# Measured numbers in a schedule's model of times, and the rows of decays loaded through ScalarE's DMA queue

## The chip, the core and the metric

The kernel runs on one core of a Trainium2 chip. The metric is the time of one execution on the device in microseconds; the value for the kernel before is the median of three runs.

## What is computed

One inference step of a hybrid decoder layer for 256 prompt tokens and 8 sample tokens, which go together as 264 columns. One input projection makes the columns of three groups of heads: windowed attention, a pooling mixer and a gated delta rule. All mixed heads go through one output projection, and a last norm follows. Cut to what bears on this case:

```python
h = rms_norm(x, norm_w)
z = h @ w_in                                   # 4096 x 14368
# delta rule, per head: decays from the cumulated gates of a chunk
gc = jnp.cumsum(chunks(g), axis=-1)
decay = jnp.exp(jnp.where(causal, gc[..., :, None] - gc[..., None, :], -jnp.inf))
a_mat = jnp.where(strict, jnp.einsum('nbhid,nbhjd->nbhij', kb, kc) * decay, 0.0)
...
qk = jnp.einsum('nbhid,nbhjd->nbhij', qc, kc) * decay
...
y = x + concat(attention, pooling, delta rule) @ w_out
return rms_norm(y, final_norm_w), new caches and states
```

The old window caches are outputs too, moved on by one row: 128 MB of them are copied from HBM to HBM.

## The kernel before

**The stream.** Both projections are one stream of 145 output tiles of 128 rows (113 of `w_in`, 32 of `w_out`), each a sum over 32 contraction tiles. A chunk is 8 contraction tiles of one output tile. Weights come as float32 from HBM into three places (`raw`) through SyncE's DMA queue, 1 MB for two chunks. Each chunk is split into two parts that TensorE multiplies at full speed: ScalarE rounds it to the upper part (`wh`), VectorE subtracts that from the original to get the lower part (`wl`). Three matmuls of 264 columns a contraction tile make the product (lines 540 to 542). `wh` and `wl` have four buffers each (HB = 4), so the splits may be three chunks ahead of TensorE; `emit_split(n + HB - 1)` follows `emit_main(n)`. The last split of a load frees its place, and the next load is then written into the program (`emit_loads`, line 456), with a piece of the caches' copy now and then (`emit_copy`).

**The side chains.** Everything else is written as Python generators: taking output tiles out of PSUM (`ev_...`), `kk` (products of the keys with themselves, one chain a head), `invert` and `assemble`, two `delta_worker`s and two `sample_worker`s (heads one after another), attention and pooling. A chain yields where it can wait. `step` (line 1395) runs once a chunk, before the chunk's matmuls: each chain may go on by one step if VectorE and ScalarE have time for it beside the stream. Products of side chains wait in a list and are put into a later chunk by `flush` (line 321), at its last contraction tile (PE_AT).

**The planner.** All this is settled when the program is built, by an estimate of the engines' clocks. `Model` (line 75) holds a time for each engine and for each column's last write and use. `Meter` (line 144) prices an instruction: fixed part, part for each element, part for a column given as a scalar (on VectorE 0.07 + 0.00104 n + 0.06 us). `emit_main` adds a price for each contraction tile to TensorE's time. The limit in `step` is

```python
end = t["pe"] + extra + (HB - 1) * 2.72 - 1.27 - MARGIN
```

A step fits if VectorE's planned time stays below `end`, and ScalarE's 1.05 us below it. The planner orders the work; on the chip the semaphores do, so a wrong price costs a wait and nothing else.

**Queues.** Each engine runs its instructions in the order in which the program was written. SyncE issues nearly all DMAs (`self.sy` and `self.ld` are the same); an issue that has to wait holds all that is behind it. `Model.dma` (line 132) prices SyncE's transfers one after the other at 359 GB/s.

**The rows of decays.** `ev_ab` writes the cumulated gates of 16 heads to a scratch tensor in HBM (`s_gc`). `load_decay(h, gcb)` (line 719) reads one row of it, 256 values, onto all 128 partitions (128 KB). It is called twice a head: in `kk`, where `due` then holds the chain until the planner takes the load for landed (`self.loaded`), and in `delta`, where four steps lie between load and use. `decay` (line 722) uses it: two instructions on VectorE, an exponential on ScalarE.

Of the kernel before, what the change touches and what calls it, by code (L numbers as in the profile page):

```python
# [11 lines left out]
P = 128  # L12
NP = 256            # prompt tokens
NB = 8              # sample tokens (one per sequence)
NT = NP + NB
NK = 32             # contraction tiles of the model width
KC = 8              # contraction tiles per chunk
# [10 lines left out]
def tile_plan():  # L28
    """Order of the output tiles of the input projection: (kind, index)."""
    plan = [("ab", 0)] + [("k", h) for h in range(CH)]  # L30
    for h in range(CH):
        plan += [("q", h), ("v", h), ("g", h)]
    for h in range(AH):
        plan += [("qa", h), ("ka", h), ("va", h), ("ga", h)]
    for g in range(4):
        plan += [("u", 2 * g), ("u", 2 * g + 1), ("gb", 2 * g), ("gb", 2 * g + 1)]
    return plan
# [37 lines left out]
class Model:  # L75
    """Estimated times (us) of the engines' queues, and of every column's last write and last use."""
# [7 lines left out]
    def span(self, ap):  # L84
        """The quarters of the partitions and the columns of a tile (the kernel's inputs and outputs are not followed)."""
        name = ap.tensor.name
        if name in self.outside:
            return None
        if name not in self.written:
            n = 1  # L90
            for x in ap.tensor.shape[1:]:
                n *= x
            self.written[name], self.used[name] = np.zeros((4, n)), np.zeros((4, n))
        dims = list(ap.ap)
        n = self.written[name].shape[1]
        if dims[0][0] % n or ap.tensor.shape[0] != P:
            return name, np.s_[:, :]
        lo, p = ap.offset % n, ap.offset // n
        last = p + dims[0][0] // n * (dims[0][1] - 1)
        hi = lo + 1 + sum(st * (c - 1) for st, c in dims[1:])  # L100
        return name, np.s_[p // 32:last // 32 + 1, lo:hi]
# [15 lines left out]
    def op(self, eng, dur, outs, ins):  # L117
        t = max(self.t[eng], self.ready(outs, ins))
        # engines take turns at a PSUM bank
        banks = {x.tensor.name for x in [*outs, *ins] if x.tensor.name in self.banks}  # L120
        for n in banks:
            last, when = self.banks[n]
            if last != eng:
                t = max(t, when + self.LAG)
        t += dur
        for n in banks:
            self.banks[n] = (eng, t)
        self.t[eng] = t
        self.done(t, outs, ins)
        return t  # L130
# [13 lines left out]
class Meter:  # L144
    """An engine, with an estimate of the time that its instructions take (us)."""
# [5 lines left out]
    def __getattr__(self, name):  # L151
        f = getattr(self.eng, name)

        def run(*a, **k):
            if name == "dma_start":
                if self.key == "sy":
                    self.b.loaded = self.b.model.dma(k["out"], k["in_"])
                return f(*a, **k)  # L158
            names = ("in_", "in0", "in1", "data0", "data1", "scalar", "scalar1", "scalar2", "scale", "bias")
            ins = [k[x] for x in names if x in k and k[x] is not None and not isinstance(k[x], (int, float))]  # L160
            ins += [x for x in a[1:] if not isinstance(x, (int, float))]
            outs = [k["out"] if "out" in k else a[0]] + ([k["accum_out"]] if "accum_out" in k else [])
            ap = (ins or outs)[0]
            n = 1
            for x in ap.shape[1:]:
                n *= x
            ptr = any(k.get(x) is not None and not isinstance(k[x], (int, float)) for x in ("scalar", "scalar1", "scale", "bias"))
            dur = self.fixed + (self.each * n if name != "reciprocal" else .0065 * n) + (self.pointer if ptr else 0.0)
            if k.get("op") == ALU.pow:
                dur = .12 + .17 * n  # L170
            self.used += dur
            t = self.b.model.op(self.key, dur, outs, ins)
            self.b.cur.ready = max(self.b.cur.ready, t)
            return f(*a, **k)  # L174
# [4 lines left out]
class Chain:  # L179
    """A generator, the estimated time at which its last step is through, and its products yet to be issued."""  # L180
# [10 lines left out]
class Builder:  # L191
# [54 lines left out]
    def get_all(self, *sizes):  # L246
        """All of them or none, so that no two chains wait for each other's space."""
        while True:
            out = []
# [40 lines left out]
    def due(self, loaded):  # L290
        """Until a load can be expected to be there."""
# [7 lines left out]
    def lose(self, t):  # L299
        """Time for ScalarE's tables."""  # L300
# [4 lines left out]
    def mm(self, out, lhsT, rhs, start=True, stop=True):  # L305
        """A side product: it is issued inside a later chunk of the stream."""
# [14 lines left out]
    def flush(self, every=True):  # L321
        """The side products whose operands can be expected to be there."""
        for c in list(self.pending):
# [7 lines left out]
            c.later = []  # L331
            self.pending.remove(c)
# [4 lines left out]
            for bufs in done:  # L337
                self.free_now(*bufs)

# [57 lines left out]
    def late_const(self):  # L397
# [4 lines left out]
        # halves: silu(z) = (tanh(z/2) + 1) * z/2  # L402
        self.ts(self.cw, self.cw, 0.5, ALU.mult)
        # buffers of the delta-rule phase
# [12 lines left out]
    def setup_stream(self):  # L417
        self.chunks = []      # (m, first k tile, number of k tiles, load index, offset in the load's tiles)
        self.loads = []       # (m, first k tile, number of k tiles, last chunk served, place, load that frees it)
# [36 lines left out]
    def emit_loads(self, limit=None):  # L456
        """The loads whose place is free."""
# [54 lines left out]
    def main_bank(self, m):  # L512
        """The PSUM bank of an output tile, and the tile that had it before."""
# [4 lines left out]
    def emit_main(self, n):  # L518
# [3 lines left out]
        for i in range(nk):  # L522
# [5 lines left out]
            self.model.t["pe"] += .226 if m == 0 else .339  # L528
            xh, xl = self.rhs(m, k)
            w = slice(i * 128, (i + 1) * 128)  # L530
            if m == 0:
                # rows 0 to 63: W's upper part by x; rows 64 to 127: its lower part by x's upper part
# [22 lines left out]
    def square_x(self, q):  # L555
        """Squares of four of the k tiles, summed into self.ssum."""
# [103 lines left out]
    def ev_ab(self, ps):  # L660
# [13 lines left out]
        # a_log -> -exp(a_log)  # L674
# [44 lines left out]
    def load_decay(self, h, gcb):  # L719
        self.ld.dma_start(out=gcb.ap, in_=self.s_gc[h:h + 1, :].to_broadcast([P, NP]))  # L720

    def decay(self, h, gcb, D):
        """D[j, t, i] = exp(gc_i - gc_j) for i >= j, else 0."""
# [58 lines left out]
    def invert(self):  # L782
        """T = (I + A)^-1 of the 128 diagonal 32 x 32 blocks, one block per partition."""
# [32 lines left out]
    def assemble(self, hb):  # L816
        """E = T^T of the 128 x 128 tiles, from its 32 x 32 diagonal blocks, in place of U."""
# [90 lines left out]
    def delta(self, h, R, kd, D, o, S, X, sq):  # L908
# [65 lines left out]
        # 128 eps (sum q^2 + eps)  # L974
# [19 lines left out]
        # the last reader of k, U and E has been issued: their place takes the head's output  # L994
# [16 lines left out]
    def sample_tab(self):  # L1011
        """Columns by (head, sequence), then rows on all partitions: e^g, k2 e^g beta, k beta."""
# [156 lines left out]
    def have(self, k, buf):  # L1169
        """Row tile k of the mixed heads; those of attention come in two parts."""  # L1170
# [202 lines left out]
    def finish_early(self):  # L1373
        """What the last norm needs of the tiles but one."""
# [20 lines left out]
    def step(self, free=False):  # L1395
        """Each side chain goes on by a step, as far as VectorE and ScalarE have time beside the stream."""
# [3 lines left out]
        end = t["pe"] + extra + (HB - 1) * 2.72 - 1.27 - MARGIN  # L1400
# [83 lines left out]
    def build(self):  # L1484
# [8 lines left out]
        # TensorE's clock rises while it is busy  # L1493
# [113 lines left out]
# the first output tiles go side by side through the contraction, while x comes in  # L1607
# [4 lines left out]
# pieces of the caches' copy per load of weights: keys' tiles, delta rule, attention, pooling, output  # L1612
# [49 lines left out]
def _bias(count):  # L1662
    """A position that `count` patterns share, as an additive term of its unscaled score."""
# [11 lines left out]
def _layouts(inp):  # L1675
# [28 lines left out]
    for n, src in (("kg", "cache_win_k"), ("vg", "cache_win_v")):  # L1704
        g = f[src][0][:, rows]                                  # (8, 320, 8, 128)
# [44 lines left out]
```

## Time and profile before

| | us |
|---|---|
| median of three runs | 1834.63 |
| lowest and highest run | 1830.6 and 1837.5 |
| span of the profiled execution, first to last instruction | 1828.2 |
| what lies between the median and the span | 6.4 |
| TensorE busy | 1801.3 (99%) |
| VectorE busy | 1298.7 (71%) |
| ScalarE busy | 850.3 (47%) |
| DMA queue of SyncE, share of 16 DMA engines | 80.5% |

The span is the profiled execution's own time on the engines; its time by the clock of the runs isn't known apart, and the median stands for it. A matmul's recorded time is longer than its place in the stream: a 264-column matmul shows 0.28 us and the next one starts 0.12 after it. So busy time alone doesn't tell whether TensorE is at its full pace; the number of matmuls in a stretch does.

### The profile page before, as it was taken

The page shows a single profiled execution, that of the slowest core. Times are in us where ns is not written, and L with a number is a line of the kernel's source. Part 1 is how long each engine was busy: PE and PEld are TensorE (multiplying, and loading weights), DVE is VectorE, ACT ScalarE, POOL GpSimd, SP SyncE. Part 2 cuts the span into 40 slices and gives each one's busy share as a digit, 9 for nine tenths or more (in the row PEclk, how much of TensorE's full clock was granted, in tenths as well). Part 3 has the DMA queues.
Part 4 walks back from the last instruction along what each step waited for, and adds up shares of the span by engine and source line. Part 5 has one row for each costly group of instructions (what it writes and reads, how often), then busy time and mean ns, then how long its engine had stood idle before and what let it go on. Part 6 is the DMA issues. An engine that isn't in the chain of part 4 may idle for free.

```text
span 1828.2 us, 38217 instructions
## 1 busy us (share of the span) xinstructions
PE 1801.3 (99%) x15120; PEld 1790.3 (98%) x15120; DVE 1298.7 (71%) x3155; ACT 850.3 (47%) x1442; POOL 192.8 (11%) x504
## 2 busy tenths in 40 slices
PE   9999999999999999999999999999999999999996
PEld 9999999999999999999999999999999999999995
DVE  7987879668789788787877778676655654444444
ACT  7644444455455455455544443434333444444442
POOL 1132560421011101111000000000000000000000
PEclk9999999999999999999999999999999999999998
DMA  9788897656787888879888888889888798888873
GB/s 322 263 289 295 272 234 260 237 198 234 262 327 269 286 305 313 304 267 319 323 312 306 313 308 297 284 283 333 306 299 288 274 339 302 295 294 303 297 240 118
DMA packets 109380, 519.66 MB, mean 284 GB/s; under 512 B 25408, under 2 KB 35872, under 8 KB 70272
## 3 DMA queue, kind: packets, MB, share of 16 engines
q1 hardware_dynamic: 108624, 516.71, 80.5%
q8 instruction: 118, 1.93, 0.4%
q0 software_dynamic: 432, 0.50, 0.1%
q14 instruction: 62, 0.51, 0.1%
q10 hardware_dynamic: 144, 0.02, 0.0%
HBM read 499.67 MB, written 152.50 MB: 357 GB/s over the span
## 4 chain that ended last, share of the span: by engine, by line
PE 88%; DVE 5%; DMA 4%; issue 1%; ACT 1%; SPq 1%; DVEq 0%; ACTq 0%
PE mps L540 27%; PE mps L541 27%; PE mps L542 27%; PE sps L307 4%; DVE arena L174 3%; DMA raw<-win 3%; DVE wl L174 2%; PE sps L311 1%; PE sps L541 1%; PE sps L540 1%; PE sps L542 1%; SPq L158 1%; DVE y L174 1%; DMA o_ds<-arena 0%; ACT wh L174 0%
## 5 line engine op out<-in xcount | busy, mean ns | idle before, releaser
L540 PE MATMUL mps<-xh,wh 128*128 128x264 f32 x3456 | 995.3, 288 | 2.0 <-ACT wh L174 2.0
L542 PE MATMUL mps<-xh,wl 128*128 128x264 f32 x3456 | 979.9, 284 | 1.7 <-DVE wl L174 1.6
L174 DVE TENSOR_TENSOR wl<-raw,wh 128x1024 fp32r<-128x1024 f32 (+1 forms) x581 | 704.5, 1214 | 389.7 <-ACT wh L174 382.4
L541 PE MATMUL mps<-xl,wh 128*128 128x264 f32 x3456 | 980.2, 284 | 0.0
L174 ACT CAST wh<-raw 128x1024 fp32r<-128x1024 f32 (+2 forms) x586 | 604.8, 1036 | 611.2 <-PE mps L541 471.7
L540 PEld LDWEIGHTS mps<-xh,wh 128*128 128x128 f32 x3456 | 652.1, 189 | 3.7 <-ACT wh L174 2.5
L541 PEld LDWEIGHTS mps<-xl,wh 128*128 128x128 f32 x3456 | 651.7, 189 | 0.2
L542 PEld LDWEIGHTS mps<-xh,wl 128*128 128x128 f32 x3456 | 648.8, 188 | 2.5 <-DVE wl L174 2.5
L174 DVE SCALAR_TENSOR_TENSOR arena<-arena 128x128 f32<-128x128 f32 (+5 forms) x882 | 264.6, 356 | 10.9 <-DMA arena<-s_k 4.2
L174 ACT ACTIVATE arena<-arena 128x128 f32<-128x128 f32 (+7 forms) x319 | 119.3, 401 | 143.3 <-DVE arena L174 140.8
L542 PE MATMUL mps<-mix,wl 128*128 128x264 f32 x512 | 145.7, 284 | 0.0
L542 PE MATMUL mps<-mixc,wl 128*128 128x264 f32 x512 | 145.7, 284 | 0.0
L540 PE MATMUL mps<-mixc,wh 128*128 128x264 f32 x512 | 145.5, 284 | 0.0
L540 PE MATMUL mps<-mix,wh 128*128 128x264 f32 x512 | 145.5, 284 | 0.0
L541 PE MATMUL mps<-mixc,wh 128*128 128x264 f32 x512 | 144.9, 283 | 0.0
L541 PE MATMUL mps<-mix,wh 128*128 128x264 f32 x512 | 144.8, 283 | 0.0
L174 POOL COPY arena<-arena 128x8 f32<-128x8 f32 (+5 forms) x192 | 67.8, 376 | 450.7 <-DVE arena L174 392.8
L540 PEld LDWEIGHTS mps<-mix,wh 128*128 128x128 f32 x512 | 96.2, 188 | 0.0
L540 PEld LDWEIGHTS mps<-mixc,wh 128*128 128x128 f32 x512 | 96.2, 188 | 0.0
L542 PEld LDWEIGHTS mps<-mixc,wl 128*128 128x128 f32 x512 | 96.1, 188 | 0.0
L542 PEld LDWEIGHTS mps<-mix,wl 128*128 128x128 f32 x512 | 96.1, 188 | 0.0
L541 PEld LDWEIGHTS mps<-mixc,wh 128*128 128x128 f32 x512 | 96.1, 188 | 0.0
(115 smaller groups left out, 1340.9 us busy)
## 6 DMA issues: line engine op xcount, KB each, us to landing
raw<-win SPq DMA_DIRECT2D x214, 1024.0 KB, 7.0
o_wk<-ck SPq DMA_DIRECT2D x128, 511.8 KB, 7.4
o_wv<-cv SPq DMA_DIRECT2D x128, 511.8 KB, 6.8
raw<-wout SPq DMA_DIRECT2D x58, 1024.0 KB, 5.3
arena<-kg SPq DMA_DIRECT2D x32, 320.0 KB, 6.7
arena<-vg SPq DMA_DIRECT2D x32, 320.0 KB, 7.1
arena<-sdT SPq DMA_DIRECT2D x32, 256.0 KB, 4.5
arena<-s_k SPq DMA_DIRECT2D x32, 256.0 KB, 4.5
```

What stands on the lines that cost most here:

```text
L158: return f(*a, **k)
L174: return f(*a, **k)
L307: self.put(lambda: self.t.matmul(out, lhsT=lhsT, rhs=rhs, start=start, stop=stop), out, [lhsT, rhs], 2)
L311: self.put(lambda: self.t.transpose(out, in_, self.ident[:k, :k]), out, [in_], 1)
L540: self.t.matmul(ps, lhsT=h[:, w], rhs=xh, start=(k == 0), stop=False)
L541: self.t.matmul(ps, lhsT=h[:, w], rhs=xl, start=False, stop=False)
L542: self.t.matmul(ps, lhsT=l[:, w], rhs=xh, start=False, stop=(k == NK - 1))
```

## The change

Besides comments and docstrings that go, the prices of the planner change, and the loads of the decays' rows move to ScalarE's queue:

- a contraction tile costs TensorE 0.3635 us in place of 0.339 (0.2415 in place of 0.226 in the first output tile), and the chunk in `step`'s limit 2.91 in place of 2.72;
- an instruction with an accumulated output costs 0.045 us more on VectorE, 0.09 on the other engines;
- a `flush` that issued anything adds 0.08 us to TensorE's time;
- `load_decay` issues on ScalarE. The planner's time of ScalarE waits for the buffer and the source and goes on by 0.06; the load is taken for landed 2.5 us later. SyncE's planned queue and the planned DMA time don't hold it any more.

```diff
@@ class Meter
             if k.get("op") == ALU.pow:
                 dur = .12 + .17 * n
+            if "accum_out" in k:
+                dur += .045 if self.key == "v" else .09
             self.used += dur
@@ def flush
+        any_issued = False
         for c in list(self.pending):
...
             c.later = []
+            any_issued = True
             self.pending.remove(c)
...
+        if any_issued:
+            self.model.t["pe"] += .08
@@ def emit_main
-            self.model.t["pe"] += .226 if m == 0 else .339
+            self.model.t["pe"] += .2415 if m == 0 else .3635
@@ def load_decay
-        self.ld.dma_start(out=gcb.ap, in_=self.s_gc[h:h + 1, :].to_broadcast([P, NP]))
+        src = self.s_gc[h:h + 1, :].to_broadcast([P, NP])
+        self.s.dma_start(out=gcb.ap, in_=src)
+        m = self.model
+        m.t["s"] = max(m.t["s"], m.ready([gcb.ap], [src])) + .06
+        self.loaded = m.t["s"] + 2.5
+        m.done(self.loaded, [gcb.ap], [src])
@@ def step
-        end = t["pe"] + extra + (HB - 1) * 2.72 - 1.27 - MARGIN
+        end = t["pe"] + extra + (HB - 1) * 2.91 - 1.27 - MARGIN
```

## Rows read from the trace of the kernel before

**Rows 1.** The page, busy time of the engines, share of the span, instructions.

```profile
PE 1801.3 (99%) x15120; PEld 1790.3 (98%) x15120; DVE 1298.7 (71%) x3155; ACT 850.3 (47%) x1442; POOL 192.8 (11%) x504
```

**Rows 2.** Table by stretches of 40 us: busy us (instructions) per engine, clock, DMA share, GB/s.

```profile
480.00:520.00 40.00, 38.55 (x317) 38.02 (x317) 34.20 (x107) 20.16 (x52) 5.74 (x15) 1.00 0.77 258
...
600.00:640.00 40.00, 37.43 (x298) 37.01 (x297) 31.27 (x91) 21.20 (x50) 4.64 (x14) 0.96 0.88 312
...
1480.00:1520.00 40.00, 40.00 (x331) 40.00 (x331) 19.92 (x21) 17.38 (x22) 0.00 (x0) 1.00 0.86 304
```

**Rows 3.** TensorE's waits, 40 to 1811 us: us in total, times, longest.

```profile
PE sps L311 <- DVE arena L174: 2.5, 3, 1.4
PE mps L540 <- ACT wh L174: 1.8, 1, 1.8
PE mps L542 <- DVE wl L174: 1.4, 2, 0.8
PE sps L307 <- DVE arena L174: 1.2, 2, 0.9
PE sps L307 <- ACT arena L174: 1.0, 1, 1.0
```

**Rows 4.** Timeline of TensorE at the largest hole: start, us, instruction, [idle before].

```profile
604.28 0.28 PE L542 MATMUL mps<-xh,wl 128*128 128x264 f32 x1
606.39 0.39 PE L540 MATMUL mps<-xh,wh 128*128 128x264 f32 x1 [1.82 <-ACT wh L174]
...
611.04 0.28 PE L542 MATMUL mps<-xh,wl 128*128 128x264 f32 x1
```

**Rows 5.** Timeline of SyncE's queue at the same place: start, us of issue.

```profile
596.11 1.84 SPq L158 DMA_DIRECT2D arena<-s_gc  x1
...
598.05 0.38 SPq L158 DMA_DIRECT2D raw<-win  x1
...
599.03 0.69 SPq L158 DMA_DIRECT2D arena<-s_gc  x1
...
599.82 0.59 SPq L158 DMA_DIRECT2D raw<-win  x1
```

**Rows 6.** Timeline of VectorE at the same place.

```profile
602.22 0.62 DVE L174 SCALAR_TENSOR_TENSOR arena<-arena 128x128 f32<-128x128 f32 x2 [3.39 <-DMA arena<-s_gc]
606.37 2.50 DVE L174 TENSOR_TENSOR wl<-raw,wh 128x1024 fp32r<-128x1024 f32 x2 [3.53 <-ACT wh L174]
```

**Rows 7.** Timeline of VectorE at 482, 506 and 595 us: pace of its instructions.

```profile
482.64 2.04 DVE L174 SCALAR_TENSOR_TENSOR arena<-arena 128x128 f32<-128x128 f32 x6
...
506.16 0.38 DVE L174 SCALAR_TENSOR_TENSOR arena<-arena 128x128 f32<-128x128 f32 x1
...
506.47 0.40 DVE L174 SCALAR_TENSOR_TENSOR arena<-arena 128x128 f32<-128x128 f32 x1
...
595.46 1.22 DVE L174 TENSOR_TENSOR wl<-raw,wh 128x1024 fp32r<-128x1024 f32 x1
596.60 1.61 DVE L174 SCALAR_TENSOR_TENSOR arena<-arena,small 128x288 f32<-128x288 f32 x3
```

**Rows 8.** Timeline of SyncE's queue, the first burst of decay loads.

```profile
126.54 6.60 SPq L158 DMA_DIRECT2D arena<-s_gc  x8
```

**Rows 9.** Loads by tile and by queue: issue ns min/median/max; KB, us to landing.

```profile
L158 SPq DMA_DIRECT2D arena<-s_gc x32: 320/572/1845, 126.5 to 825.4; - x32
...
arena<-s_gc SPq DMA_DIRECT2D x32, 128.0 KB, 9.0
...
arena<-scT POOLq DMA_DIRECT2D x2, 96.0 KB, 6.7
```

**Rows 10.** Timeline of ScalarE's queue at the start.

```profile
0.74 0.40 ACTq L158 DMA_DIRECT2D small<-nw  x1
```

**Rows 11.** Waits of ScalarE and of SyncE's queue: us in total, times, longest.

```profile
ACT wh L174 <- PE mps L541: 471.7, 283, 3.4
...
SPq L158 <- DMA o_ds<-arena: 136.9, 26, 10.5
```

## The prediction

> **What bounds the kernel now.** I read the page first: TensorE is busy 99% of the span [rows 1], so time can only come from places where its stream of matmuls stops. The table by stretches says how fast the stream is when nothing disturbs it: 331 matmuls in 40 us, 0.1208 us each, so a chunk of 8 contraction tiles (24 matmuls) takes 2.90 us; and it says where matmuls are missing: 317 in 480 to 520, 298 in 600 to 640 [rows 2]. The list of TensorE's waits after the start-up and before the end names what stopped it: 2.5 + 1.8 + 1.4 + 1.2 + 1.0 = 7.9 us in nine waits; 4.7 of it are side products waiting for their operands (sps), 3.2 are the main stream waiting for the halves of the weights (mps) [rows 3]. These idle times count from the modelled end of a matmul, 0.28 us after its start where the next one could start after 0.12, so each hides 0.16 more: 9 x 0.16 = 1.4 us.
>
> The largest hole is at 604. From 604.28 to 611.04 there are 18 steps that should take 18 x 0.12 = 2.2 us and take 6.8: 4.6 us lost [rows 4], of which about 1.6 us is the granted clock: after TensorE had stood idle there it ran at 1.2 instead of 2.4 GHz (0.96 as the mean of 600 to 640 [rows 2], so 0.04 x 40 x 2 = 3.2 us at half speed). So all that a better schedule could win inside the stream is 7.9 + 1.4 + 1.6 = 10.9 us, 0.6% of the time. Start and end are not touched by the change.
>
> Why the hole is there is read from SyncE's queue and VectorE. SyncE issues two loads of decays in it, at 596.11 (1.84 us of issue) and at 599.03 (0.69), each directly in front of a load of weights [rows 5]. VectorE waits 3.39 us for the second one and only goes on at 602.22; ScalarE and the next splits of weights stand behind that [rows 6]. The load of weights at 598.05 could have left when the split that freed its place was through, at 596.60 [rows 7]: it left 1.45 us late.
>
> **The change, part by part.** *Time of a matmul in the schedule's model* (0.339 to 0.3635 us a contraction tile, 2.712 to 2.908 a chunk; in the limit of `step`, 2.72 to 2.91). The measured chunk is 2.90, so the new number is right and the old one 6.5% short. The old error was a hidden reserve: per chunk the planner gave VectorE 2.712 - 1.135 (its price of a split) = 1.58 us of side work, and now gives 2.908 - 1.135 = 1.77; and VectorE may be planned 3 x 0.19 = 0.57 us further ahead. It adds no instruction.
>
> *Accumulating instructions* get 0.045 us more on VectorE and 0.09 on ScalarE. The planner priced an accumulating 128-column product at 0.07 + 0.133 = 0.203, now 0.248; the trace has them 0.31 apart. The form with a column as its scalar stays at 0.263; six of them take 2.04, 0.34 each; a split takes 596.60 - 595.46 = 1.14 [rows 7]. A chunk planned full of accumulating products was 7.8 x 0.31 + 1.14 = 3.56 us of real work and becomes 7.1 x 0.31 + 1.14 = 3.34; one full of the other form was 6.0 x 0.34 + 1.14 = 3.18 and becomes 6.7 x 0.34 + 1.14 = 3.42. All of them exceed 2.90. So the model stays too quick for VectorE, better in one form and worse in the other. What hides this is that few chunks are full: VectorE is busy 34.2 of 40 us in one of its denser stretches [rows 2].
>
> *0.08 us for each group of side products*: it moves TensorE's planned time and no instruction, by less than the 0.19 a chunk above. I put it and the first tile's 0.226 to 0.2415 at nothing of their own.
>
> Together these three reorder the steps of the side chains. Bounds: they remove all waits for side operands, -4.7 us [rows 3], or they double them, +4.7. The planned margin of VectorE shrinks by 0.57 us while half of its prices remain too low, so I take +1.0, on the loss side and nearer to zero.
>
> *Loads of decays through ScalarE's queue.* 32 transfers of 128 KB move. SyncE no longer issues them: 0.57 us median each, up to 1.85 [rows 9]; what stands behind them there (loads of weights, pieces of the cache copy, stores of the sample state) leaves earlier. Where nothing else holds SyncE this costs or gains nothing, since a load of weights is issued some chunks ahead. In the hole at 604 it counts: the load of weights leaves 1.45 us earlier, and VectorE's 3.39 us wait goes, since the decay was issued behind a queue that waits for stores of the sample state. If both go, the first main wait (1.8 us) shrinks to some 0.5, and the second and the low clock go with it: 4.6 - 0.6 = 4.0 us won. Bounds 0 (another load falls into the same place) and -4.6. I take -4.0, because both waits of that row end at a decay load or at what stands behind one. Next late there is the same load of weights, landing at 603.8 instead of 605.2.
>
> On ScalarE each issue is an instruction of its own queue: the only one in the trace takes 0.40 us [rows 10], on SyncE eight in a row take 6.60 [rows 8]; the planner charges 0.06. It also waits there for the last reader of its buffer, with the next split of weights (wh) queued behind it, which VectorE's split and then TensorE wait for. In the delta phase the buffer was last written by ScalarE itself, so there is no wait. The burst at 126.54, eight loads in one step, blocks ScalarE for 8 x 0.40 = 3.2 to 6.6 us. The cover is the ring of four chunks: three of them, less a split on each of the two engines at 1.14, 8.7 - 2.3 = 6.4 us at its fullest. ScalarE has idle time of its own, 471.7 us spent waiting only for TensorE to free a place [rows 11]. Bounds 0 and +3 (half the cover already used); I take +0.5.
>
> *A landing time of 2.5 us*, counted from the issue, in place of the planner's whole queue. The only landing that a waiting instruction shows is 602.22 - 599.03 = 3.2 us [rows 5, 6]; the median on SyncE's queue is 9.0, on GpSimd's own queue 6.7 [rows 9]. At 3.2 VectorE waits 0.7 us for each of the 16 loads of the keys' phase, and each is covered by the 6.4 us of the ring: 0. At 6.7 it waits 4.2 us for each of the 8 loads that follow the burst one tile (4 chunks, 11.6 us) apart, has some 1.7 us to spare in a tile (5.8 of 40 as in the dense stretch [rows 2]), and loses 2.5 x 8 - 6.4 = 13.6 us. I take 0, from the row of the same transfer; +13.6 stays as the other end.
>
> **Sum.** Against the profiled execution: -4.0 + 1.0 + 0.5 = -2.5 us on its span of 1828.2, so 1825.7. The median of the runs lies 6.4 us above the span (1834.63); I add the same 6.4: 1832.
>
> The Trainium skill, page "DMA: Bandwidth & Descriptors", section "Issuing engines are not separate DMA queues", says that transfers started by different engines share the same 16 DMA engines and interleave, and that spreading them saves only the time to issue them. By it the decays meet the weights again on the DMA engines, and 1.45 us of issue is what is left of the 4.0; the sum would be 1834.6. No load in this trace shows it either way, since ScalarE's only transfer is at the start.
>
> **Rivals.**
> *All waits go.* An exact clock for TensorE places every side product where its operands are ready, and SyncE is freed: -10.9 us, 1824. For it: the waits of the largest hole share one cause. Against it: the model still prices VectorE's work too low, and SyncE is held far longer by stores of the sample state (136.9 us [rows 11]) than by decays.
> *Only the issue time is saved.* The decays compete on the DMA engines with the weights, or the reordered schedule meets another late load: -1.45 + 1.5, 1834.7. For it: DMA share 0.88 in 600 to 640 [rows 2].
> *VectorE is packed too densely* (the slower side). Place: the delta and sample phase, 440 to 830. A chunk filled with the column form really takes 3.42, 0.52 us over the stream's 2.90; the ring's 6.4 us are used up after 6.4 / 0.52 = 12 full chunks in a row, and from there TensorE loses 0.52 us a chunk. With 40 full chunks it is 28 x 0.52 = 14.6 us, and the holes lower the clock besides: 1849. Against it: VectorE is at 86% in the dense stretch, so a run of more than 12 full chunks needs the side chains to bunch up.
> *Decays land late* (6.7 us): 1832 + 13.6 = 1845.6. For it: the stream's loads of weights share the DMA engines with them; against it: the 3.2 us above were measured in their midst.
>
> **How the numbers follow.** Forecast 0.50 (own range 1826 to 1839), all waits gone 0.13, issue time only 0.16, VectorE too dense 0.15, late decays 0.06. 0.5% is 9.2 us, about what a measurement of this kernel can tell from no change: faster is below 1825.5, slower above 1843.8. Faster: the first rival and the edge of the forecast, 0.14. Slower: the dense VectorE and half of the late decays, 0.18 (the other half, partly covered, stays within). Within: 0.68. The range 1823 to 1848 takes in the first rival and the late decays and leaves out most of the dense case.
>
> **What would show it.** Right: no s_gc on SyncE, TensorE's waits in mid-stream at 5 to 9 us instead of 7.9 plus a clock below 1, no wait of VectorE on s_gc over 1 us, ScalarE's issues at 0.4 to 0.8 us each. Wrong: VectorE's waits on s_gc adding up to tens of us before 230; the table by stretches missing more than 30 matmuls in several stretches between 440 and 830 with VectorE near 100% there; a gap of ScalarE's splits at the first burst that reaches TensorE.

## The result, and the profile after

The change makes the kernel slower: 1913.60 us (median, runs from 1910.05 to 1918.29) against 1836.07 us of the kernel before on the same chip, a ratio of 1.0422 with a 95% interval of 1.0402 to 1.0441. The forecast of 1832 us had the wrong sign, and its range ended at 1848. The profiled span grew from 1828.2 to 1908.5 us, 80.3 us. (A run's time lies 1.7 to 2.1 us above its own span wherever both are on record, so the profiled execution of the kernel before was one of its quick ones, at some 1830 us; that is why the spans differ by more than the medians.)

**Is work added?** No: the page after has the same 15120 matmuls, and VectorE and ScalarE are as long busy as before [rows 1]. TensorE is 24 us longer busy with the same count, which goes with the lower clock below.

```profile
PE 1825.3 (96%) x15120; PEld 1807.1 (95%) x15120; DVE 1303.9 (68%) x3155; ACT 848.7 (44%) x1442; POOL 183.7 (10%) x504
```

**Where is the time lost?** The table by stretches of 40 us: busy us (instructions) of PE, PEld, DVE, ACT, POOL, then granted clock, DMA share, GB/s.

```profile
120.00:160.00 40.00, 36.04 (x284) 35.61 (x283) 29.67 (x65) 19.01 (x29) 5.57 (x19) 0.96 0.74 259
...
200.00:240.00 40.00, 35.60 (x281) 35.00 (x280) 28.67 (x88) 14.43 (x20) 17.86 (x46) 0.96 0.60 200
480.00:520.00 40.00, 37.84 (x299) 37.38 (x298) 32.37 (x110) 21.68 (x57) 4.41 (x15) 0.96 0.81 289
...
600.00:640.00 40.00, 36.76 (x289) 36.19 (x288) 32.10 (x99) 19.04 (x44) 5.20 (x16) 0.96 0.77 263
720.00:760.00 40.00, 31.46 (x251) 30.85 (x250) 28.86 (x95) 15.54 (x32) 2.71 (x10) 0.96 0.67 210
1480.00:1520.00 40.00, 40.00 (x326) 39.74 (x325) 25.63 (x47) 17.99 (x33) 0.00 (x0) 1.00 0.72 240
```

The kernel before, in three of these stretches that [rows 2] doesn't have:

```profile
120.00:160.00 40.00, 40.00 (x335) 40.00 (x334) 32.12 (x80) 20.14 (x30) 6.24 (x23) 1.00 0.88 314
...
200.00:240.00 40.00, 40.00 (x335) 40.00 (x335) 34.56 (x100) 17.59 (x24) 19.90 (x49) 1.00 0.76 266
...
720.00:760.00 40.00, 40.00 (x335) 40.00 (x334) 29.55 (x80) 20.16 (x41) 4.49 (x12) 1.00 0.84 309
```

Matmuls are missing from 120 us on: 51 of 335 in 120 to 160, 84 of 335 in 720 to 760. The stretch 1480 to 1520 is no loss: it holds the work that the kernel before does some 80 us earlier, at 1400 to 1440, and there too 326 matmuls run in 40 us. In none of the poor stretches shown is VectorE or the DMA full: VectorE is busy 29 to 32 of 40 us, the DMA at most 0.81. The engines wait for each other.

**For what does TensorE wait?** The waits between start-up and end (us in total, times, longest), which answer to [rows 3].

```profile
PE sps L309 <- DVE arena L176: 28.0, 18, 6.2
PE sps L313 <- DVE arena L176: 11.3, 9, 2.9
PE sps L309 <- ACT arena L176: 11.2, 8, 2.8
PE mps L546 <- ACT wh L176: 6.9, 2, 3.6
PE mps L548 <- DVE wl L176: 2.4, 3, 0.9
PE sps L309 <- POOL arena L176: 2.0, 1, 2.0
PE mps L547 <- issue: 1.1, 1, 1.1
```

62.9 us in 42 waits, where 7.9 in nine were; 52.5 of it are side products (sps) that were written into TensorE's program before their operands are there. With 33 x 0.16 us hidden in the 33 added waits (5.3), and the clock, which fell to 0.96 in many stretches after such stops (0.986 over the span against 0.995: 0.014 x 1908.5 - 0.005 x 1828.2 = 17.6 us at half speed), this estimate gives 55.0 + 5.3 + 17.6 = 77.9 of the 80.3 us.

**Why are the operands late?** The chain of waits through the worst stretch, 720 to 760, in order of time (start, us, what), from the point where it leaves VectorE.

```profile
731.80 1.73 DVE arena L176 x9
733.76 5.87 DMA arena<-s_gc
739.64 0.52 SPq L158
740.21 0.57 SPq L158
740.88 0.38 SPq L158
741.30 9.09 DMA o_ds<-arena
750.45 0.33 SPq L158
750.82 4.85 DMA arena<-s_k
755.78 0.16 DVE arena L176
...
758.02 0.80 PE sps L309 x2
```

SyncE stands until a load of decays has landed (5.87 us; ScalarE issued it). Then come a piece of the cache copy, an output, a load of weights and a store of a sample head's state. The next head's state goes into the place that the store reads, so its load waits for the store (9.09 us), the row of k stands behind it (4.85 us), VectorE waits for that, and TensorE for VectorE's product. Of the 26 us from 731.80 on, 19.8 are landings. The planner's price from issue to landing of such a transfer, 256 KB on an idle queue, is 0.65 + 256 KB at 359 GB/s (0.73) + 0.9 = 2.3 us.

The first two stops, at 144.34 and 233.89, come from decays that land late. VectorE waits for them (its timeline):

```profile
142.29 0.61 DVE L176 SCALAR_TENSOR_TENSOR arena<-arena 128x128 f32<-128x128 f32 x2 [4.54 <-DMA arena<-s_gc]
...
231.84 0.61 DVE L176 SCALAR_TENSOR_TENSOR arena<-arena 128x128 f32<-128x128 f32 x2 [3.46 <-DMA arena<-s_gc]
```

ScalarE stands behind VectorE for 7.64 and 6.30 us, splits the next weights late, and TensorE waits 3.21 and 3.65 us for ScalarE's half (`wh`) and 0.75 each for VectorE's. The second of these decays lands 5.66 us after its issue; the planner counted 2.5. The stretches 120 to 160 and 200 to 240 lose 51 and 54 matmuls, some 105 x 0.1208 = 12.7 us.

Over the whole span SyncE's queue waits for decays, which it doesn't in the kernel before, and VectorE for decays and the rows of k (second fence).

```profile
SPq L158 <- DMA arena<-s_gc: 41.0, 12, 8.9
```

```profile
DVE arena L176 <- DMA arena<-s_k: 26.6, 13, 5.7
DVE arena L176 <- DMA arena<-s_gc: 14.6, 5, 4.5
```

The issues themselves are short on ScalarE (ns, min/median/max), at the median below the 0.40 us that was foreseen [rows 10]:

```profile
L158 ACTq DMA_DIRECT2D arena<-s_gc x32: 325/327/1451, 103.7 to 870.4; - x32
```

### The profile page after: what moved, and what is told of

The parts are those of the page before. It is cut to its first block, busy times and chain, and to the rows that moved or that the text cites. A ratio compares the mean times of both kernels' runs of the same rounds, so it can differ in the third digit from the quotient of the medians.

```text
span 1908.5 us, 38246 instructions
## 1 busy us (share of the span) xinstructions
PE 1825.3 (96%) x15120; PEld 1807.1 (95%) x15120; DVE 1303.9 (68%) x3155; ACT 848.7 (44%) x1442; POOL 183.7 (10%) x504
## 4 chain that ended last, share of the span: by engine, by line
PE 59%; DVE 13%; DMA 10%; issue 2%; ACT 2%; POOL 1%; SPq 1%; DVEq 0%; ACTq 0%; POOLq 0%
PE mps L546 19%; PE mps L547 19%; PE mps L548 18%; DVE arena L176 8%; DVE wl L176 4%; PE sps L309 3%; DMA raw<-win 3%; DMA arena<-s_k 2%; DMA o_ds<-arena 2%; ACT wh L176 1%; DMA arena<-s_gc 1%; DMA s_q<-small 1%; POOL arena L176 1%; SPq L158 1%; DMA arena<-spT 1%
## 5 line engine op out<-in xcount | busy, mean ns | idle before, releaser
L546 PEld LDWEIGHTS mps<-xh,wh 128*128 128x128 f32 x3456 | 658.9, 191 | 8.6 <-ACT wh L176 7.3
L548 PEld LDWEIGHTS mps<-xh,wl 128*128 128x128 f32 x3456 | 655.4, 190 | 5.8 <-DVE wl L176 4.5
L176 DVE SCALAR_TENSOR_TENSOR arena<-arena 128x128 f32<-128x128 f32 (+6 forms) x882 | 265.2, 358 | 49.1 <-DMA arena<-s_k 26.6
L176 ACT ACTIVATE arena<-arena 128x128 f32<-128x128 f32 (+6 forms) x319 | 117.7, 400 | 218.6 <-DVE arena L176 218.2
L176 POOL COPY arena<-arena 128x3 f32<-128x3 f32 (+5 forms) x192 | 61.7, 343 | 510.4 <-DVE arena L176 398.1
```

What stands on the lines that cost most here:

```text
L546: self.t.matmul(ps, lhsT=h[:, w], rhs=xh, start=(k == 0), stop=False)
L548: self.t.matmul(ps, lhsT=l[:, w], rhs=xh, start=False, stop=(k == NK - 1))
```

## Experiments

Each difference is that of the medians to the kernel before, measured beside it on the same chip; the interval is that of the ratio.

| run | what | median, us | difference | ratio, 95% interval |
|---|---|---|---|---|
| e1_pe | TensorE's exact time alone | 1892.35 | +51.0 | 1.0238 to 1.0308 |
| e2_decay | `load_decay` alone | 1865.07 | +23.8 | 1.0085 to 1.0168 |
| e3_small | accumulating and flush prices alone | 1860.15 | +18.8 | 1.0068 to 1.0127 |
| e4_slack | after, side products 1 us later | 1907.51 | +66.2 | 1.0319 to 1.0389 |
| p1_margin | before, MARGIN 2.02 | 1852.77 | +13.1 | 1.0041 to 1.0093 |
| p2_vfixed | before, VectorE's fixed price 0.0705 | 1853.70 | +14.0 | 1.0057 to 1.0094 |
| e5_queue | before's order, decays on ScalarE's queue | 1859.99 | +20.3 | 1.0087 to 1.0122 |
| e6_sp | after's order, decays on SyncE's queue | 1929.05 | +89.4 | 1.0469 to 1.0503 |
| e7_pool | before's order, decays on GpSimd's queue | 1841.48 | +1.2 | 0.9991 to 1.0020 |
| e14_after_pool | after's order, decays on GpSimd's queue | 1924.51 | +86.2 | 1.0453 to 1.0511 |
| e8_reserve | e1, VectorE's share a chunk as before | 1880.07 | +39.8 | 1.0203 to 1.0239 |
| e9_margin | e1, MARGIN 3.5 | 1885.80 | +45.5 | 1.0233 to 1.0266 |
| e10_low | TensorE's time 7% shorter still | 1896.40 | +56.1 | 1.0291 to 1.0322 |
| e11_dma | e1, DMA prices 7% dearer | 1853.02 | +14.8 | 1.0049 to 1.0096 |
| e12_nocopy | before without the cache copy | 1822.13 | -16.1 | 0.9899 to 0.9944 |
| e13_nocopy_pe | e1 without the cache copy | 1835.59 | -2.7 | 0.9981 to 1.0004 |
| e15_after_dma | after, DMA prices 7% dearer | 1865.63 | +30.1 | 1.0129 to 1.0180 |
| e16_dma305 | e1, DMA at 305 GB/s | 1831.75 | -3.8 | 0.9963 to 0.9989 |

### Which part costs it

**e1_pe, e2_decay, e3_small**: each part alone, in the kernel before. In the expectations, A blames TensorE's price, B the loads of decays.

```diff
# e1_pe
-.226 if m == 0 else .339        ... (HB - 1) * 2.72
+.2415 if m == 0 else .3635      ... (HB - 1) * 2.91
# e2_decay: the new load_decay alone
# e3_small: the accum_out price and the 0.08 us of flush alone
```

> The kernel before with the prices of TensorE alone changed: a contraction tile 0.3635 (first tile 0.2415), 2.91 a chunk in the limit of step. Theory A (TensorE's planned clock no longer lags, so flush puts side products into the stream before their operands are there, as VectorE's prices and the landing times are still too low): 1890 to 1915 us, TensorE waiting 40 us or more for side products' operands where the kernel before waits 5. Theory B (the moved decay loads do it: late landing and waits between the queues): 1830 to 1845 us.

> The kernel before with load_decay alone changed: the row of decays through ScalarE's queue, landed 2.5 us later in the planner. Theory A: 1825 to 1845 us. Theory B: 1880 us or more, with VectorE and SyncE waiting for the decays.

> The kernel before with the two small prices alone: 0.08 us for a group of side products on TensorE, 0.045 and 0.09 for an accumulated output. Theory A: 1835 to 1850 us, since 0.08 a group makes TensorE's planned clock a little later and the accumulated outputs work against it. Theory B: no change, 1830 to 1840.

The three numbers for TensorE cost 51.0 us alone, as A said; this is the part that the forecast priced at +1.0. Their profile has the waits for side operands of the changed kernel, 42.4 us (TensorE's waits of e1_pe):

```profile
PE sps L307 <- DVE arena L174: 14.8, 14, 2.3
PE sps L311 <- DVE arena L174: 13.7, 11, 2.8
PE sps L307 <- ACT arena L174: 9.0, 9, 1.6
PE sps L311 <- ACT arena L174: 4.9, 1, 4.9
```

The decays cost 23.8, more than A and less than B expected, and on the wrong side of the forecast's -3.5 (-4.0 + 0.5). e3_small, at 18.8, lies above the ranges of both. The parts add up to 93.6, more than the whole 77.5; that they meet the same waits is likely, but not shown.

**e4_slack**: after, with a group of side products put in only when its operands are planned to be there 1 us ahead.

```diff
-PE_SLACK = 0.0
+PE_SLACK = -1.0
```

> The changed kernel, with a side product put into the stream only if the planner has its operands ready 1 us before TensorE's planned time (PE_SLACK -1.0 in place of 0). Theory A: TensorE's waits for side products fall from 53 us to under 25, time 1850 to 1880. Theory B: the operands are late by the landing of loads, 3 us and more, so 1 us changes little: 1895 to 1915.

Waits for side operands stayed at 52.4 us, and the time, 1907.51, lies in B's range. So the products are not just a little too early; A in this form fell.

### What an empty edit costs

**p1_margin, p2_vfixed**: two edits of the kernel before that are too small to mean anything by themselves and only make the planner choose otherwise in places.

```diff
# p1_margin
-MARGIN = 2.0
+MARGIN = 2.02
# p2_vfixed
-Meter(self, "v", nc.vector, .07, ...
+Meter(self, "v", nc.vector, .0705, ...
```

> The kernel before with MARGIN 2.02 in place of 2.0: no price is more right or more wrong, but the steps fall in another order. Theory A (TensorE's exact clock makes the rest late): 1830 to 1845 us. Theory C (the old order is a chosen low one, and any other order of such a planner is slower): 1850 us or more.

> The kernel before with VectorE's fixed price 0.0705 in place of 0.07 us. Theory A: 1830 to 1845 us. Theory C: 1850 us or more.

Both cost 13 to 14 us: the order of the kernel before is a fortunate (or a picked) one. In p2_vfixed most of it is a single wait of TensorE for a bank that VectorE still holds, at 473 us (e3_small has one of 9.3 us alike):

```profile
PE mps L540 <- DVE arena L174: 11.9, 1, 11.9
```

So of e1's 51 us some 14 may be no more than the loss of that order, and e3's 18.8 are hardly more. Two edits are a small sample, and it is no fixed price: e16_dma305 below has another order and loses nothing. Some 37 us need a cause.

### The queue of the decays

**e5_queue, e6_sp**: the queue without the planner, and the planner without the queue.

```diff
# e5_queue: in before; the planner still prices it in SyncE's queue
-self.ld.dma_start(out=gcb.ap, in_=...)
+self.nc.scalar.dma_start(out=gcb.ap, in_=src)
+self.loaded = self.model.dma(gcb.ap, src)
# e6_sp: in after
-self.s.dma_start(out=gcb.ap, in_=src)
+self.nc.sync.dma_start(out=gcb.ap, in_=src)
```

> The kernel before with the decays issued on ScalarE's queue and nothing else: the planner still counts them in SyncE's queue, so VectorE, TensorE and GpSimd keep their order. If the queue itself costs (waits between the two queues, late landing): 1850 us or more. If it only saves SyncE's issue time, as the prediction had it: 1830 to 1842, with the hole at 604 smaller than 4.6 us.

> The changed kernel with the decays back in SyncE's queue and its planner as it is, so the order of the other work is that of the changed kernel. If the queue costs: under 1895 us. If the new order costs (the planner's numbers): 1905 to 1920.

In e5_queue TensorE, VectorE and GpSimd have before's order, instruction by instruction, and the move alone costs 20.3 us. SyncE's queue first, then ScalarE's, at the first burst of decays in e5_queue:

```profile
117.51 0.66 SPq L158 DMA_DIRECT2D o_wk<-ck  x1
133.38 0.35 SPq L158 DMA_DIRECT2D o_cv<-arena  x1
133.87 0.33 SPq L158 DMA_DIRECT2D arena<-scT  x1
135.08 0.33 SPq L158 DMA_DIRECT2D raw<-win  x1
...
130.39 3.71 ACTq L721 DMA_DIRECT2D arena<-s_gc  x8
```

SyncE issues nothing from 118.17 to 133.38. In the kernel before the same three DMAs leave at 118.39, 118.84 and 120.46:

```profile
118.39 0.35 SPq L158 DMA_DIRECT2D o_cv<-arena  x1
118.84 0.39 SPq L158 DMA_DIRECT2D arena<-scT  x1
120.46 0.33 SPq L158 DMA_DIRECT2D raw<-win  x1
```

The store `o_cv` shares no data with the decays. The program's own list of waits says what ties them:

```
SyncE    75 DMA o_cv<-arena 128x88 [waits DMAHW3, Pool]
SyncE    76 DMA arena<-scT 128x192 [waits DMAHW4, DMASW1]
SyncE    77 DMA raw_81<-win 128x2048 [waits DMAHW5, DVE]
ScalarE 137 DMA arena<-s_gc 128x256 [waits DMAHW0]
```

All DMAs of SyncE and ScalarE report their landing on one set of eight semaphores (DMAHW0 to 7), dealt out in turn in the order of the program, and a DMA waits for the landing of the one that had its semaphore last. On one queue that is eight places back and mostly landed. On two queues, SyncE's next DMAs wait until ScalarE has come to the burst in its own order (130.39), issued it and seen it land. SyncE's waits for decays in e5_queue, 79.8 us where the kernel before has none:

```profile
SPq L158 <- DMA arena<-s_gc: 79.8, 17, 15.1
```

These waits reach TensorE. The chain into its first stop (144.03) runs from ScalarE's issue over the landing of a decay (131.24, 3.77 us) to SyncE, SyncE's next load of weights (135.08, 7.77 us), ScalarE's split and TensorE. The chain into its longest stop (4.41 us, 624.52) has a decay's landing that holds SyncE (596.06, 7.80 us), then a store of the sample state, and again a load of weights. ScalarE itself waits only 5.1 us for decays.

e6_sp went the other way, to 1929.05, above both ranges that were expected: in the new order the decays are worse off on SyncE's queue, since the plan takes them for landed 2.5 us after a free ScalarE; VectorE waits for them, up to 8.1 us at a time:

```profile
DVE arena L176 <- DMA arena<-s_gc: 39.7, 9, 8.1
```

**e7_pool**: GpSimd's DMAs have semaphores of their own (DMASW).

```diff
-self.ld.dma_start(out=gcb.ap, in_=...)
+self.nc.gpsimd.dma_start(out=gcb.ap, in_=src)
+self.loaded = self.model.dma(gcb.ap, src)
```

> The order of the kernel before on TensorE, VectorE and ScalarE, with the 32 loads of decays issued on GpSimd's queue and the planner unchanged. On ScalarE's queue the same move cost 20 us, and SyncE's queue waited 15.1 us at a time for a decay to land. Theory of shared completion semaphores (SyncE's and ScalarE's DMAs take turns on one set of eight, GpSimd's have a set of their own): no wait of SyncE's queue on a load of decays, other than for data, and 1830 to 1846 us. Rival (a decay that leaves SyncE's order meets the loads of weights on the DMA engines, whoever issues it): again 1853 to 1865 us. Rival (GpSimd is late to issue, its own work stands ahead): waits of VectorE on decays of over 20 us, above 1850.

The 20 us are gone (+1.2), and decays are not among SyncE's waits. The same transfers meet the same weights on the DMA engines, so contention is not the cause. It is ScalarE's queue, and the chains of e5_queue name the shared semaphores as what stops TensorE in the order of before; what ScalarE's own issues (32 x 0.33 = 10.5 us in all) add was not tried apart.

**e14_after_pool**: the same in the changed kernel.

```diff
-self.s.dma_start(out=gcb.ap, in_=src)
+self.nc.gpsimd.dma_start(out=gcb.ap, in_=src)
```

> The changed kernel in its own order, with the 32 loads of decays issued on GpSimd's queue in place of ScalarE's. Theory that the queue's 20 us add up with the rest: 1885 to 1900 us, no wait of SyncE's queue on a decay. Rival (in this order other waits take the place): 1905 to 1920.

SyncE no longer waits for decays, and yet the time is 1924.51, above the ranges of both. As the rival had it, other waits take the place, those for a landing that was planned at 2.5 us; on VectorE:

```profile
DVE arena L176 <- DMA arena<-s_gc: 37.5, 8, 8.5
```

All of them lie before 280 us. From 120 to 280 us TensorE starts 1024 matmuls here, 1211 in the changed kernel and 1339 in the kernel before: at 0.1208 us each, some 38 of the 86.2 us are lost there, and some 15 of the 77.5 in the changed kernel.

### Why the exact TensorE time costs 51 us

The first theory was a lost reserve: the too quick TensorE clock had kept VectorE's chunks emptier.

**e8_reserve, e9_margin, e10_low**: VectorE's share restored, its distance enlarged, and TensorE's time made still shorter.

```diff
# e8_reserve: e1 and, in emit_split
+self.model.t["v"] += .196 * nk / KC
# e9_margin: e1 and
-MARGIN = 2.0
+MARGIN = 3.5
# e10_low: in before
-.226 if m == 0 else .339        ... (HB - 1) * 2.72
+.2105 if m == 0 else .315       ... (HB - 1) * 2.52
```

> The kernel before with the three numbers for TensorE (0.3635, 0.2415, 2.91), which alone cost 51 us, and 0.196 us more of VectorE's planned time for each chunk's split, so that a chunk gives the side chains 1.58 us of VectorE again as before, not 1.77. Theory of the lost reserve (the exact price lets the planner fill VectorE's and ScalarE's chunks until real delays have no slack): 1840 to 1860 us, TensorE's waits for side operands under 20 us. Rival (the exact price is bad for another reason, such as side products placed nearer to their operands or DMA times planned too early): 1875 to 1895 us, waits of 35 us or more.

> The kernel before with the three numbers for TensorE and MARGIN at 3.5 in place of 2.0: VectorE and ScalarE are planned 1.5 us less far ahead of TensorE, but a chunk still gives them 1.77 us. Theory of the lost reserve in its form 'too little distance': 1840 to 1865. In its form 'too much side work a chunk': distance helps less, 1865 to 1890. Rival (neither): 1885 to 1900.

> The kernel before with TensorE's numbers a further 7% too low (0.315, 0.2105, 2.52): a chunk gives the side chains 1.39 us of VectorE. Theory of the lost reserve: any wait that is left gets less, 1830 to 1853 us, where the upper part is what any reshuffling of the order costs. Rival (the price of before was tuned and every change of it costs according to its size): 1875 or more. Also possible: the side chains fall behind the stream so far that the last heads come late for the output projection; then one long wait near 1430 us.

The theory fell: the restored reserves bring back 11 and 5.5 of 51 us. e10_low is slow for another reason, two long stops that end at 813 and 1123 us, where TensorE waits for a side chain that fell behind the stream (into the first run a store of the sample state, 10.90 us, a load of the row of k, 3.63 us, and VectorE's work on it). TensorE's waits:

```profile
PE sps L307 <- DVE arena L174: 33.5, 3, 30.0
PE sps L311 <- DVE arena L174: 21.9, 2, 17.4
```

The second theory came from the chain through 720 to 760: the plan's DMA is too quick. Median us from issue to landing in the kernel before, against the planner's 4.5 for the first and 2.3 for the others on an idle queue:

```profile
raw<-win SPq DMA_DIRECT2D x214, 1024.0 KB, 7.0
arena<-s_k SPq DMA_DIRECT2D x32, 256.0 KB, 4.5
...
o_ds<-arena SPq DMA_DIRECT2D x32, 256.0 KB, 9.5
```

The planner's queue adds waiting under load too, so these rows alone don't give the size of the error. A TensorE clock 7% too quick made every DMA, counted in chunks, 7% dearer; the exact time took that away.

**e11_dma**: e1 with the DMA prices made dearer by the same share.

```diff
 # e1 and, in Model.dma
-... + .46   ... t + .65) + max(n / 359e3, .02)     ... + .9
+... + .493  ... t + .697) + max(n / 334.9e3, .021) ... + .965
```

> The kernel before with the three exact numbers for TensorE, and the planner's DMA prices 7% dearer too (335 GB/s in place of 359; 0.493 an issue, landing 0.965). Theory of the DMA price (the old TensorE time hid that DMA was priced too cheap): 1850 to 1868 us, the sample phase again about as long as before, SyncE's waits on stores of the sample state back near 137 us from 197. Rival (TensorE's price itself, or any order that isn't that of before, costs the 51): 1880 to 1900.

1853.02: 36 of the 51 us are back (51.0 - 14.8), and what remains is the size of p1 and p2. One part of the expectation missed: SyncE's waits on stores of the sample state did not fall (204.7 us, 197.4 in e1_pe). They don't go with the time from run to run either (136.9 in the kernel before, 104.4 in the changed kernel), so the store in the chain through 720 to 760 stands for late DMAs, not for all of the loss. What fell are TensorE's waits for side operands, from 42.4 to 11.1 us:

```profile
PE sps L307 <- DVE arena L174: 7.1, 6, 2.2
...
PE sps L307 <- ACT arena L174: 2.9, 4, 1.2
PE sps L311 <- DVE arena L174: 1.1, 2, 0.8
```

**e12_nocopy, e13_nocopy_pe**: the transfers relieved in place of the plan. The cache copy isn't issued; the planner still prices it, so each order stays as it was.

```diff
 # emit_copy, in before and in e1
-self.sy.dma_start(out=..., in_=...)
+self.loaded = self.model.dma(..., ...)
```

> The kernel before, with its plan and order, without the 256 pieces of the caches' copy (128 MB that this kernel doesn't move; the planner still prices them). All theories: the DMA share falls from 0.8 to about 0.55, and the few waits of TensorE shrink: 1815 to 1836 us. It is the base for the same run with the exact TensorE time.

> The kernel before with the three exact numbers for TensorE (51 us slower with the copy), without the pieces of the caches' copy. Theory of the DMA price: with the queue relieved the difference to the run without copies in the old order falls to 0 to 18 us. Rival (VectorE and ScalarE, or the order of the side products, are late by themselves): the difference stays at 35 us or more.

Without the copy the exact time costs 13.5 us instead of 51.0 in the very same order of the compute engines. TensorE's waits for side operands in e13_nocopy_pe are 9.9 us in eleven waits, for 42.4 in e1_pe.

Two ways, another plan and fewer transfers, agree: some 37 of the 51 us (36.2 and 51.0 - 13.5 = 37.5) come from DMAs that are later than the plan has them. That they agree to 1 us is luck, since an empty edit alone moves the time by 13. And without the copy SyncE has 256 issues less as well, so the second way doesn't part the DMA engines from SyncE's queue.

**e15_after_dma, e16_dma305**: the dearer DMA in the changed kernel, and a still dearer one.

```diff
 # e15_after_dma: in after, the diff of e11_dma; e16_dma305: e11_dma and
-n / 334.9e3
+n / 305e3
```

> The changed kernel with the planner's DMA prices 7% dearer (335 GB/s, 0.493 an issue, landing 0.965); the decays stay on ScalarE's queue. Theory that the DMA price is what the exact TensorE time uncovered: the same 39 us as in the kernel before come back, 1865 to 1885 us. Rival (here the decays, which are planned to land in 2.5 us and held by no queue, set the loss): 1895 or more, with VectorE's waits on decays at 15 us or more as now.

> The kernel before with the exact TensorE time and a DMA price of 305 GB/s, 0.493 an issue, landing 0.965. If the DMA price is the quantity that counts, a still slower queue in the plan leaves fewer waits: 1830 to 1850 us, and it may beat the kernel before. Rival (335 was enough, what remains is the cost of an order that was not picked): 1848 to 1865.

In the changed kernel 47 of 77.5 us come back (77.5 - 30.1), at the low end of what was expected. Of what is left SyncE's waits for decays (42.7 us) are a likely part; no run joins the dearer DMA with another queue for the decays there. With 305 GB/s the exact TensorE time is no loss at all: 1831.75, 0.24% below the kernel before (ratio 0.9976, an interval that just excludes 1), with decays left on SyncE's queue. The stores of the sample state tell what changed (issue ns, first to last start, first e1_pe, then e16_dma305):

```profile
L158 SPq DMA_DIRECT2D o_ds<-arena x32: 337/572/892, 395.2 to 967.6; - x32
```

```profile
L158 SPq DMA_DIRECT2D o_ds<-arena x32: 332/572/1641, 397.6 to 1139.5; - x32
```

The 32 state stores are spread over 742 us instead of 572 (562 in the kernel before, which is about as quick, so a wider spread isn't the only way), and TensorE meets seven waits in mid-stream, 9.2 us. Which of the four DMA prices matters most was not tried apart, nor were other rates between and beyond.

## Why the prediction was wrong, step by step

- **What bounds the kernel** held: all of the loss is stops in TensorE's stream, and start and end did not move. But the argument "all that can be won is 10.9 us" said nothing about what can be lost, and no row of before bounds that.
- **The term +1.0 for the planner's new prices failed: TensorE's three numbers alone measured +51.0.** Its bounds, the waits removed or doubled (-4.7 to +4.7), took the waits that are left in a good order for a measure of what a new one can bring. The step "the old error was a hidden reserve" was right, but the prediction saw it on VectorE: VectorE's reserve given back is worth 11 us (e8_reserve), the DMA's price 36 (e11_dma), each with the luck of one new order in it. Rows that hint at it were there: landings of 9.0 and 6.7 us [rows 9], waits of SyncE for state stores of 136.9 us [rows 11].
- **A new order** was given no price of its own. The accumulating and flush prices, part of the same +1.0, cost 18.8 alone, and the empty edits p1 and p2 cost 13.1 and 14.0. This rival wasn't among the prediction's.
- **"SyncE no longer issues them ... what stands behind leaves earlier", -4.0, failed in sign.** It leaves later: with the move alone SyncE waits 79.8 us for decays (e5_queue, +20.3). The list of queues that the step was to consider had SyncE's and ScalarE's own order, not the semaphores that they share.
- **ScalarE's issues**, +0.5 from 0.40 us each: measured 0.327 at the median, 3.71 for the burst of eight in e5_queue. Right in size; what the burst stopped there was SyncE.
- **Landing of 2.5 us, taken at 0 with +13.6 as the other end.** The other end was the nearer one: two late decays in the keys' phase stop TensorE at 144 and 234 us, some 12.7 us. The form differs, two stops with a low clock and not eight loads of 2.5 us each. One quick landing of 3.2 [rows 5, 6] was a poor choice; the median on ScalarE's queue was 4.3 in e5_queue, and the second of the two took 5.66.
- **The rule of the Trainium skill**, page "DMA: Bandwidth & Descriptors", section "Issuing engines are not separate DMA queues", that another engine saves issue time only: by it the move is near nothing. The trace agrees on GpSimd's queue (+1.2), where nothing ties the queues. On ScalarE's it differs by 20 us, and the measurement decides.
- **The 6.4 us added at the end** are no fixed distance: a run lies 1.7 to 2.1 us above its own span. That moved the forecast by some 4 us and isn't what failed.
- **The rivals.** "VectorE packed too densely" named the right sign and the stretch of most of the loss (more than 30 matmuls are missing in several pieces of 440 to 830), but its signature, VectorE near 100%, is not there (29 to 32 of 40 us). "Decays land late" is a part: its 13.6 us are about what the two first stops cost, not the 77.5. Of the signs of being right, no load of s_gc on SyncE came true; TensorE's waits of 5 to 9 us (62.9), no wait of VectorE on a decay over 1 us (up to 4.5) and ScalarE's issues at 0.4 to 0.8 us (0.327) did not.

## What to carry to other kernels

A planner's prices are a set: an error in one can be what makes another bearable, so correct the price of the bottleneck together with that of what it waits for (here the DMA), and look at landings under load, not at one idle transfer. Before a DMA is moved to another engine's queue, list which semaphores its landing shares with the old queue; the order of the two programs is then tied together. And where the order of work is picked by a planner, measure an empty change or two first: here they cost 13 and 14 us, and only a difference well above that speaks for a reason.

## What the runs showed of the hardware

In the kernel before, where the DMA moved 284 GB/s on average and the queue's share was 80.5%, a load of 256 KB took 4.5 us from issue to landing at the median and a store of 256 KB 9.5. With TensorE's stops its granted clock was 0.96 as the mean of 40 us in the five losing stretches of the changed kernel that are shown (a part of each at 1.2 instead of 2.4 GHz); in others, as 440 to 480 with 306 matmuls for 336, it stayed at 1.00. Without the cache copy the DMA moved 212 GB/s, and TensorE's waits nearly vanished in the old order (1.6 us).
